# Strided attention scores of the odd layer: 64 by 64 tiles per head and class instead of 128-row products with zeros, and a row minimum taken in two steps

## The chip, the cores and the metric

The kernel runs on one core of a Trainium2 chip. The metric is the device time of one execution, in microseconds (us). Below, PE is the matrix engine (TensorE), DVE the vector engine, ACT the scalar engine, POOL GpSimd, and SP the queue that issues most DMAs. PSUM is the memory that PE writes; it is used here as eight banks of 128 partitions by 512 floats, four under the name `acc` and four under the name `w`.

## The reference

The network has two layers over 256 tokens of width 1024; each layer is a mixer followed by a squared-ReLU MLP, with RMS norms. The change is in the odd layer's mixer, a mixture of three dilated windows with 16 heads of width 64. Cut to what matters:

```
DIL_PAIRS = ((128, 1), (512, 4), (2048, 16))      # window, step; 3 groups
hcat = (xn @ w_in).reshape(b, s, 3, 3, 16, 64)    # group, q/k/v, head
q, k = rope(hcat[:, :, :, 0]), rope(hcat[:, :, :, 1]);  v = hcat[:, :, :, 2]
for each group g and token i:                     # keys i + offset, in steps of 1, 4, 16
    sc = q_g[i] . k_g[keys] * 64**-0.5            # keys outside 0..255 are masked
    o_g, lse_g = softmax(sc) @ v_g[keys], logsumexp(sc)
out = sum over g of softmax_g(lse_g) * o_g        # then out @ w_o
```

Because the three groups are mixed by their softmax denominators, one softmax over the keys of all three groups together gives the same result. That is how the kernel computes it.

## The kernel before

**Units.** Function `odd` goes over eight units, two heads each (j = 0 and 1). For a unit, `qk_steps` computes six 128-row products (q and k of the three groups, 64 rows per head) with the weights split in two float32r parts (`split`: ACT casts `whi`, DVE subtracts `wlo`, L201 and L202; `mm3`, L205 to L207, runs three products per weight tile), `rope` rotates them on ACT (L931, L932) and DVE (L934 to L944), and `value_steps` computes v. `attention` then computes scores and softmax, and `mix` (L1000, L1005) multiplies with v.

**Order of tokens.** The 256 tokens stand in an order in which the 64 tokens of equal residue modulo 4 follow each other, and in these 64 the four residues modulo 16. A token's keys in group 1 (step 4) and in group 2 (step 16) are therefore all in its own block of 64 tokens, called a class here. There are four classes: `i` (a tile of 128 queries) times `c` (a half of it).

**Scores.** For each (i, j) one bank `ss[i, j]` of kind `w` takes 384 columns: 256 of group 0 (`two_heads`, L214, two float32r products of 64 rows beside each other) and 128 of groups 1 and 2 (L967). For the latter, `q12` holds group 1 in partitions 0 to 63 and group 2 in 64 to 127. So that one product over 128 rows keeps the groups apart, `k12` is stored as a block diagonal with zeros in its other blocks: 64 columns of group 1, then 64 of group 2. Its two buffers are zeroed once by POOL (L877), and DVE writes the two blocks in two instructions (L944). L967 is a plain float32 product, as are L1000, L1005 and L283: each such matmul of the program stands in the trace as two MATMUL records. A form such as 128\*64 in a row is the part of the array that the product takes, rows by columns; 128x128 behind it is the moving operand, partitions by columns.

**Softmax.** For each (i, j) DVE adds the mask, scales, and takes the row's minimum of the negated scores in one instruction of 384 columns (L974, followed by the short record that reads its accumulator), ACT takes the exponential with the sum (L976), DVE the reciprocal (L977), and ACT scales (L978). `turn` transposes the 384 probabilities in three blocks on PE (L985, into a `w` bank), and ACT or DVE copies them out (L987).

**What sets the order.** `weave` interleaves the steps of one unit's attention with the projections of the next; in it the scores of unit u - 1 come first, then `other()`, which is `mix` of unit u - 2, then pauses, then the four turns between the projections' steps. Unit 0 and unit 7 have no `mix` behind their scores. Inside each engine's queue the framework's scheduler chooses the order from its own costs. The weights come through SP's queue, which waits for free buffers. The MLP after the odd layer follows `hand_over`.

Of the kernel before, what the change touches and what calls it, by code (L numbers as in the profile page):

```python
# [19 lines left out]
F32 = mybir.dt.float32  # L20
F32R = mybir.dt.float32r
AF = mybir.ActivationFunctionType
ALU = mybir.AluOpType
# [26 lines left out]
def trunk(ctx, tc, a, out):  # L50
# [100 lines left out]
    def cut(j, i, n):  # L151
        w = specs[j][1] // n
        return slice(i * w, (i + 1) * w)
# [55 lines left out]
    def two_heads(o, hi, lo, ts):  # L209

        for n, (y, z) in enumerate(((hi, hi), (hi, lo), (lo, hi))):
            for j in range(2):
                pb = slice(64 * j, 64 * j + 64)
                nc.tensor.matmul(o[j], y[pb, 0, ts], z[pb, 1, :], start=n == 0, stop=n == 2)  # L214
# [10 lines left out]
    def tok(t):  # L225
        return slice(t * P, (t + 1) * P)
# [638 lines left out]
    def odd(op, xT, s, late):  # L865
        xh, xl = xT
        cosT = op.tile([P, T], F32, name="cosT")
        sinT = op.tile([P, T], F32, name="sinT")
        mask = op.tile([P, NT, 384], F32, name="mask")
        for dst, nm in ((cosT, "cos_f"), (sinT, "sin_f"), (mask, "dil_mask")):  # L870
            nc.sync.dma_start(dst, a[nm])
        mixed = [quarter_pair("oa"), quarter_pair("ob")]

        k12 = []
        for i in range(2):
            z = op.tile([P, 2, 4, P], F32, name=f"k12_{i}")
            nc.gpsimd.memset(z, 0.0)  # L877
            k12.append(z)

        def unit_tiles(u):  # L880
            d = {"k12": k12[u % 2]}
            for n, shape, dt in (("q0h", [P, 2, T], F32R), ("q0l", [P, 2, T], F32R), ("q12", [P, 2, T], F32),
                                 ("v0", [P, NT, P], F32), ("v12", [P, 4, P], F32)):
                d[n] = op.tile(shape, dt, tag=n, name=n, bufs=2)
            return d

        def value_steps(d):

            wt, acc = [], {}

            def gemm(i, half):
                if len(wt) <= half:
                    wt.append(weight())
                first = i not in acc
                if first:
                    acc[i] = bank("acc")
                pq = acc[i]
                wh, wl = wt[half]
                for k in range(4):
                    ws = slice(k * 384, k * 384 + 384)  # L900
                    kk = 4 * half + k
                    mm3(pq[:, 0:384], xh[:, kk, tok(i)], xl[:, kk, tok(i)], wh[:, ws], wl[:, ws], first and k == 0, not first and k == 3)
            def out(i):
                pq, ri = acc[i], column(r[0], i)
                nc.vector.tensor_scalar(d["v0"][:, i, :], pq[:, 0:P], ri, None, ALU.mult)
                for c in range(2):
                    rows = slice(64 * c, 64 * c + 64)
                    nc.scalar.activation(d["v12"][0:64, 2 * i + c, :], pq[rows, P:2 * P], AF.Copy, scale=ri[rows])
                    nc.scalar.activation(d["v12"][64:P, 2 * i + c, :], pq[rows, 2 * P:3 * P], AF.Copy, scale=ri[rows])

            return [lambda i=i, h=h: gemm(i, h) for i in range(NT) for h in range(2)], [lambda i=i: out(i) for i in range(NT)]

        def qk_steps(d):


            hold = {}

            def gemm(b, f, half):
                if f == 0 and half == 0:
                    hold["w"], hold["p"] = weight(), bank("acc")  # L920
                (wh, wl), pq = hold["w"], hold["p"]
                for k in range(4 * half, 4 * half + 4):
                    ws = slice((f * KT + k) * P, (f * KT + k + 1) * P)
                    mm3(pq[:, f * T:(f + 1) * T], wh[:, ws], wl[:, ws], xh[:, k, :], xl[:, k, :], k == 0, k == KT - 1)
                if f == 1 and half == 1:
                    rope(b, pq)

            def rope(b, pq):
                sw, r1 = scratch([512], "sw"), scratch([2, T], "r1")
                for r in range(0, P, 64):  # L930
                    nc.scalar.copy(sw[r:r + 32], pq[r + 32:r + 64])  # L931
                    nc.scalar.copy(sw[r + 32:r + 64], pq[r:r + 32])  # L932
                sw = sw.rearrange("p (f n) -> p f n", f=2)
                nc.vector.tensor_tensor(r1, pq.rearrange("p (f n) -> p f n", f=2), cosT.unsqueeze(1).broadcast_to([P, 2, T]), op=ALU.mult)  # L934
                nc.vector.tensor_tensor(sw, sw, sinT.unsqueeze(1).broadcast_to([P, 2, T]), op=ALU.mult)
                if b == 0:
                    nc.vector.tensor_tensor(r1, r1, sw, op=ALU.add)
                    split(d["q0h"], d["q0l"], r1)
                elif b == 1:
                    nc.vector.tensor_tensor(d["q12"], r1, sw, op=ALU.add)  # L940
                else:
                    for r in (0, 64):
                        cut = lambda z: z[r:r + 64].rearrange("p j (c n) -> p j c n", n=64)
                        nc.vector.tensor_tensor(d["k12"][r:r + 64, :, :, r:r + 64], cut(r1), cut(sw), op=ALU.add)  # L944

            return [lambda v=(b, f, h): gemm(*v) for b in range(3) for f in range(2) for h in range(2)]

# [2 lines left out]
            return [g[0], lambda: run_all([g[1], o[0]]), g[2], lambda: run_all([g[3], o[1]])]  # L950

        turned = {}

        def attention(u, d, other, pause=2):


            probs = {}

            def scores():
                ss = {(i, j): bank("w") for i in range(NT) for j in range(2)}  # L960
                for i in range(NT):
                    two_heads([ss[i, j][:, 0:T] for j in range(2)], d["q0h"], d["q0l"], tok(i))
                for i in range(NT):
                    for j in range(2):
                        for c in range(2):
                            rows = slice(64 * c, 64 * c + 64)
                            nc.tensor.matmul(ss[i, j][rows, T:T + P], d["q12"][:, j, i * P + 64 * c:i * P + 64 * c + 64],  # L967
                                             d["k12"][:, j, 2 * i + c, :], start=True, stop=True)
                other()
                for i in range(NT):  # L970
                    for j in range(2):
                        sn, pp = scratch([384], "sn"), scratch([384], "pp")
                        mn, z, rz = (work.tile([P, 1], F32, tag=v, name=v, bufs=4) for v in ("dmn", "dz", "drz"))
                        nc.vector.tensor_tensor_reduce(out=sn, in0=ss[i, j][:, 0:384], in1=mask[:, i, :], op0=ALU.add, op1=ALU.min,  # L974
                                                       scale=-(HD ** -0.5), scalar=3e38, accum_out=mn)
                        nc.scalar.activation(pp, sn, AF.Exp, bias=mn, scale=-1.0, accum_out=z)  # L976
                        nc.vector.reciprocal(rz, z)  # L977
                        nc.scalar.activation(pp, pp, AF.Copy, scale=rz)  # L978
                        probs[i, j] = pp

            def turn(i, j):
                pp = probs.pop((i, j))
                pt = bank("w")
                for b in range(3):
                    nc.tensor.transpose(pt[:, b * P:(b + 1) * P], pp[:, b * P:(b + 1) * P], ident)  # L985
                pts = turned[u, i, j] = op.tile([P, 3, P], F32, tag="pts", name="pts", bufs=6)
                nc.any.tensor_copy(out=pts, in_=pt[:, 0:384].rearrange("p (b n) -> p b n", b=3))  # L987

            wait = lambda: None
            return [scores] + [wait] * pause + [f for i in range(NT) for j in range(2) for f in (lambda i=i, j=j: turn(i, j), wait)]  # L990
# [74 lines left out]
def _constants():  # L1065
    con = {}
    con["cos_r"], con["sin_r"] = _tables(32, ORDER)
    con["cos_f"], con["sin_f"] = (np.ascontiguousarray(np.tile(z.transpose(1, 0, 2).reshape(T, HD).T, (2, 1)))
                                  for z in _tables(HD, ORDER))
    q = ORDER.reshape(NT, P)  # L1070
    own = ORDER.reshape(4, 64).repeat(64, axis=0).reshape(NT, P, 64)
    ok0 = np.abs(q[:, :, None] - ORDER[None, None, :]) <= 64
    d = q[:, :, None] - own
    ok1 = (d % 4 == 0) & (np.abs(d) <= 256)
    ok2 = (d % 16 == 0) & (np.abs(d) <= 1024)
    m = np.where(np.concatenate([ok0, ok1, ok2], 2), 0.0, NEG).astype(np.float32)
    con["dil_mask"] = np.ascontiguousarray(m.transpose(1, 0, 2))
    return con

# [57 lines left out]
```

## Time and profile before

| | us |
|---|---|
| median of 3 runs | 737.83 (737.17 to 737.85) |
| the profiled execution, its time | 738.17 |
| its span | 736.4 |
| PE busy in the span | 727.2 (99%) |
| PE weight loads | 680.7 (92%) |
| DVE, ACT, POOL busy | 610.5 (83%), 558.9 (76%), 79.9 (11%) |
| the odd layer's strided scores, PE records of L967 | 128 records, 8.8 us |
| their softmax minimum, DVE L974 | 32 instructions, 17.5 us |
| writing k of groups 1 and 2, DVE L944 | 16 instructions, 10.9 us |

A row of the timeline gives the start, the time, the engine, the line, the operation, the tiles and how many records were merged; a bracket at its end names idle time before it and what ended that. Records of PE overlap, since matmuls are pipelined: the time from the start of one row to the start of the next is what a row costs. The granted clock of PE is 1.00 throughout the odd layer.

### The profile page before, as it was taken

The page shows a single profiled execution, that of the slowest core. Times are in us where ns is not written, and L with a number is a line of the kernel's source. Part 1 is how long each engine was busy: PE and PEld are TensorE (multiplying, and loading weights), DVE is VectorE, ACT ScalarE, POOL GpSimd, SP SyncE. Part 2 cuts the span into 40 slices and gives each one's busy share as a digit, 9 for nine tenths or more (in the row PEclk, how much of TensorE's full clock was granted, in tenths as well). Part 3 has the DMA queues.
Part 4 walks back from the last instruction along what each step waited for, and adds up shares of the span by engine and source line. Part 5 has one row for each costly group of instructions (what it writes and reads, how often), then busy time and mean ns, then how long its engine had stood idle before and what let it go on. Part 6 is the DMA issues. An engine that isn't in the chain of part 4 may idle for free.

```text
span 736.4 us, 14008 instructions
## 1 busy us (share of the span) xinstructions
PE 727.2 (99%) x5442; PEld 680.7 (92%) x5442; DVE 610.5 (83%) x1090; ACT 558.9 (76%) x1027; POOL 79.9 (11%) x75
## 2 busy tenths in 40 slices
PE   9999999999999999999999999999999999999996
PEld 6988899999999998999999999999999999999995
DVE  6888859999999959887778677776759999999957
ACT  7778968767766756888988989889867768767752
POOL 0100002224212000000000000000003123322000
PEclk9999999999999999999999999999999999999998
DMA  8773338798999643644443444534558699898611
GB/s 312 275 263 131 115 115 216 227 288 236 263 266 261 194 145 150 226 146 140 173 160 144 156 151 171 176 129 160 199 204 216 208 275 262 247 263 249 190 52 57
DMA packets 34178, 143.78 MB, mean 195 GB/s; under 512 B 3776, under 2 KB 5312, under 8 KB 25024
## 3 DMA queue, kind: packets, MB, share of 16 engines
q1 hardware_dynamic: 26208, 127.94, 49.6%
q0 software_dynamic: 7616, 14.68, 12.0%
q8 instruction: 42, 0.69, 0.4%
q10 hardware_dynamic: 288, 0.28, 0.1%
q14 instruction: 24, 0.20, 0.1%
HBM read 141.84 MB, written 1.05 MB: 194 GB/s over the span
## 4 chain that ended last, share of the span: by engine, by line
PE 92%; DVE 4%; ACT 1%; issue 1%; DMA 1%; POOL 0%; SPq 0%; POOLq 0%; DVEq 0%
PE acc L205 17%; PE acc L206 16%; PE acc L207 16%; PE w L205 11%; PE w L206 11%; PE w L207 11%; PE w L214 1%; PE w L985 1%; DVE wlo L202 1%; PE w L801 1%; PE w L967 1%; PE acc L1000 1%; PE w L815 1%; ACT whi L201 1%; DVE xl L242 1%
## 5 line engine op out<-in xcount | busy, mean ns | idle before, releaser
L202 DVE TENSOR_TENSOR wlo<-raw,whi 128x512 fp32r<-128x512 f32 (+3 forms) x360 | 297.0, 846 | 56.0 <-ACT whi L201 55.6
L201 ACT CAST whi<-raw 128x512 fp32r<-128x512 f32 (+3 forms) x360 | 253.8, 745 | 89.4 <-PE w L206 64.8
L206 PE MATMUL w<-xl,whi 128*128 128x256 f32 x528 | 149.6, 283 | 0.1
L207 PE MATMUL w<-xh,wlo 128*128 128x256 f32 x528 | 149.3, 283 | 0.0
L205 PE MATMUL w<-xh,whi 128*128 128x256 f32 x528 | 148.9, 283 | 0.0
L205 PE MATMUL acc<-xh,whi 128*128 128x256 f32 x432 | 125.2, 290 | 0.0
L206 PE MATMUL acc<-xl,whi 128*128 128x256 f32 x432 | 122.3, 283 | 0.0
L207 PE MATMUL acc<-xh,wlo 128*128 128x256 f32 x432 | 122.3, 283 | 0.0
L206 PEld LDWEIGHTS w<-xl,whi 128*128 128x128 f32 x528 | 101.2, 192 | 1.6 <-DVE xl L242 0.6
L205 PEld LDWEIGHTS w<-xh,whi 128*128 128x128 f32 x528 | 101.0, 192 | 1.0
L207 PEld LDWEIGHTS w<-xh,wlo 128*128 128x128 f32 x528 | 101.2, 192 | 0.0
L140 POOL COPY sum<-sum 128x512 f32<-128x512 f32 x28 | 41.4, 1494 | 468.3 <-DVE wlo L202 271.9
L205 PEld LDWEIGHTS acc<-xh,whi 128*128 128x128 f32 x432 | 82.5, 191 | 1.3 <-issue 0.3
L206 PEld LDWEIGHTS acc<-xl,whi 128*128 128x128 f32 x432 | 82.5, 191 | 0.0
L207 PEld LDWEIGHTS acc<-xh,wlo 128*128 128x128 f32 x432 | 82.4, 191 | 0.0
L205 PE MATMUL acc<-whi,xh 128*128 128x384 f32 (+2 forms) x160 | 55.4, 348 | 0.2 <-ACT whi L201 0.2
L206 PE MATMUL acc<-wlo,xh 128*128 128x384 f32 (+2 forms) x160 | 55.1, 344 | 0.4 <-DVE wlo L202 0.4
L207 PE MATMUL acc<-whi,xl 128*128 128x384 f32 (+2 forms) x160 | 54.7, 342 | 0.0
L201 ACT CAST hh<-h 128x896 fp32r<-128x896 f32 (+1 forms) x32 | 28.9, 903 | 18.2 <-DVE h L378 17.2
L205 PE MATMUL w<-whi,hh 128*128 128x512 f32 (+1 forms) x108 | 42.1, 390 | 0.0
L206 PE MATMUL w<-wlo,hh 128*128 128x512 f32 (+1 forms) x108 | 41.5, 384 | 0.0
L207 PE MATMUL w<-whi,hl 128*128 128x512 f32 (+1 forms) x108 | 41.2, 382 | 0.0
(225 smaller groups left out, 1495.4 us busy)
## 6 DMA issues: line engine op xcount, KB each, us to landing
raw<-in_w SPq DMA_DIRECT2D x36, 1024.0 KB, 5.4
raw<-in_w_oqk SPq DMA_DIRECT2D x24, 1024.0 KB, 4.8
raw<-in_w SPq DMA_DIRECT2D x28, 768.0 KB, 5.3
sum<-in_w POOLq DMA_DIRECT2D x28, 512.0 KB, 8.5
raw<-in_w_ov SPq DMA_DIRECT2D x16, 768.0 KB, 4.3
sum<-in_w SPq DMA_DIRECT2D x28, 256.0 KB, 6.1
raw<-in_w_oe SPq DMA_DIRECT2D x4, 1024.0 KB, 6.6
raw<-in_w_oo SPq DMA_DIRECT2D x4, 1024.0 KB, 4.8
```

The lines of the kernel that those rows point to most:

```text
L140: nc.gpsimd.tensor_copy(out=sums[:, 1, :], in_=sums[:, 0, :])
L201: a = nc.scalar.copy(hi, src).ins
L202: return a, (eng or nc.vector).tensor_tensor(lo, src, hi.bitcast(F32), op=ALU.subtract).ins
L205: nc.tensor.matmul(o, sh, mh, start=first, stop=False)
L206: nc.tensor.matmul(o, sh, ml, start=False, stop=False)
L207: nc.tensor.matmul(o, sl, mh, start=False, stop=last)
L214: nc.tensor.matmul(o[j], y[pb, 0, ts], z[pb, 1, :], start=n == 0, stop=n == 2)
L242: lambda: nc.vector.scalar_tensor_tensor(lo, v, gk, hi.bitcast(F32), ALU.mult, ALU.subtract).ins)
L801: nc.tensor.transpose(pt[:, b * P:(b + 1) * P], pp[:, b // 2, (b % 2) * P:(b % 2 + 1) * P], ident)
L815: nc.tensor.matmul(pvo[64 * j:64 * j + 64, 0:P], v[:, kk, h * 64:(h + 1) * 64], pts[:, 2 * j + kk, :], start=kk == 0, stop=kk == NT - 1)
L967: nc.tensor.matmul(ss[i, j][rows, T:T + P], d["q12"][:, j, i * P + 64 * c:i * P + 64 * c + 64], d["k12"][:, j, 2 * i + c, :], start=True, ...
L985: nc.tensor.transpose(pt[:, b * P:(b + 1) * P], pp[:, b * P:(b + 1) * P], ident)
```

## The change

The zeros are gone: `k12` becomes a tile like `q12` (group 1 in partitions 0 to 63, group 2 in 64 to 127, two buffers), written by one DVE instruction, and POOL's two memsets are dropped. The score of one class, head and group is a product of its own, 64 rows by 64 columns with a moving operand of 64 columns: 16 matmuls per unit where 8 were. The rows of the array that a product takes follow the group g, the columns follow c. Products of g = 0 go to bank `ss[i, 0]`, those of g = 1 to `ss[i, 1]`, whichever head they are of, at columns 0 to 63 for head 0 and 320 to 383 for head 1; group 0's scores move to columns 64 to 319. So head j's scores stand in 320 neighbouring columns of its own bank (256 of group 0 and one class block), and 64 more in the other head's bank. The minimum is taken in two steps: one instruction over the 320 columns, whose result `m0` is the starting value of a second one over the 64. The mask grows from 384 to 640 columns, so that both heads' orders are windows of it, and the places of groups 1 and 2 in v and the order of the three transposed blocks follow.

```diff
-        mask = op.tile([P, NT, 384], F32, name="mask")
+        mask = op.tile([P, NT, 640], F32, name="mask")
...
-        k12 = []
-        for i in range(2):
-            z = op.tile([P, 2, 4, P], F32, name=f"k12_{i}")
-            nc.gpsimd.memset(z, 0.0)
-            k12.append(z)
...
-                    for r in (0, 64):
-                        cut = lambda z: z[r:r + 64].rearrange("p j (c n) -> p j c n", n=64)
-                        nc.vector.tensor_tensor(d["k12"][r:r + 64, :, :, r:r + 64], cut(r1), cut(sw), op=ALU.add)
+                    nc.vector.tensor_tensor(d["q12" if b == 1 else "k12"], r1, sw, op=ALU.add)
...
+        END = (slice(0, 64), slice(320, 384))
...
-                    two_heads([ss[i, j][:, 0:T] for j in range(2)], d["q0h"], d["q0l"], tok(i))
+                    two_heads([ss[i, j][:, 64:64 + T] for j in range(2)], d["q0h"], d["q0l"], tok(i))
                 for i in range(NT):
                     for j in range(2):
                         for c in range(2):
-                            rows = slice(64 * c, 64 * c + 64)
-                            nc.tensor.matmul(ss[i, j][rows, T:T + P], d["q12"][:, j, i * P + 64 * c:i * P + 64 * c + 64],
-                                             d["k12"][:, j, 2 * i + c, :], start=True, stop=True)
+                            ts = slice(i * P + 64 * c, i * P + 64 * c + 64)
+                            for g in range(2):
+                                pb = slice(64 * g, 64 * g + 64)
+                                nc.tensor.matmul(ss[i, g][64 * c:64 * c + 64, END[j]], d["q12"][pb, j, ts], d["k12"][pb, j, ts],
+                                                 start=True, stop=True)
...
-                        nc.vector.tensor_tensor_reduce(out=sn, in0=ss[i, j][:, 0:384], in1=mask[:, i, :], op0=ALU.add, op1=ALU.min,
-                                                       scale=-(HD ** -0.5), scalar=3e38, accum_out=mn)
+                        low = 3e38
+                        for b, c, at, m in ((j, slice(64 * j, 64 * j + 320), slice(64 - 64 * j, 384 - 64 * j), m0), (1 - j, END[j], END[j], mn)):
+                            nc.vector.tensor_tensor_reduce(out=sn[:, at], in0=ss[i, b][:, c], in1=mask[:, i, T - T * j:640 - T * j][:, at], op0=ALU.add, op1=ALU.min,
+                                                           scale=-(HD ** -0.5), scalar=low, accum_out=m)
+                            low = m
...
-                for b in range(3):
-                    nc.tensor.transpose(pt[:, b * P:(b + 1) * P], pp[:, b * P:(b + 1) * P], ident)
+                for b, at in enumerate((0, P, T) if j else (P, T, 0)):
+                    nc.tensor.transpose(pt[:, b * P:(b + 1) * P], pp[:, at:at + P], ident)
```

In the built program the lines behind the change stand a few numbers lower: L967 becomes L962, L974 becomes L972, L976 to L978 become L975 to L977, L985 becomes L984, L987 becomes L986, L1000 and L1005 become L999 and L1004.

PE's queue keeps every other instruction at its place. At the scores of unit 1, followed by `mix` of unit 0, it stood before:

```order
L214 MATMUL w<-q0l,q0h 128x256 x2
L214 MATMUL w<-q0h,q0l 128x256 x2
L967 MATMUL w<-k_1_3458,q_3467 64x128 x8
L1000 MATMUL acc<-pts,v_3463 64x128 x4
L1005 MATMUL acc<-pts,v_3464 64x64 x4
L1000 MATMUL acc<-pts,v_3463 64x128 x4
L1005 MATMUL acc<-pts,v_3464 64x64 x4
L205 MATMUL acc<-xh,whi 128x256
```

And now (`k` and `q` are the tiles k12 and q12, `w` the score banks):

```order
L214 MATMUL w<-q0l,q0h 128x256 x2
L214 MATMUL w<-q0h,q0l 128x256 x2
L962 MATMUL w<-k_3465,q_3464 64x64 x16
L999 MATMUL acc<-pts,v_3460 64x128 x4
L1004 MATMUL acc<-pts,v_3461 64x64 x4
L999 MATMUL acc<-pts,v_3460 64x128 x4
L1004 MATMUL acc<-pts,v_3461 64x64 x4
L205 MATMUL acc<-xh,whi 128x256
```

Sixteen matmuls of 64 columns stand where eight of 128 stood.

DVE's queue at the softmax of unit 7, before (`wlo` are parts of the next weights, `ISA` with a 128x1 result reads the accumulator):

```order
L202 TENSOR_TENSOR wlo<-raw,whi 128x512 x4
L974 ISA sn,dmn<-w,mask 128x384
L974 ISA dmn 128x1
L202 TENSOR_TENSOR wlo<-raw,whi 128x512
L974 ISA sn,dmn<-w,mask 128x384
L974 ISA dmn 128x1
L977 RECIPROCAL drz<-dz 128x1
```

And now:

```order
L202 TENSOR_TENSOR wlo<-raw,whi 128x512 x5
L972 ISA sn,dm_6820<-w,mask 128x320
L972 ISA dm_6820 128x1
L972 ISA sn,dmn<-w,mask,dm_6820 128x64
L972 ISA dmn 128x1
L972 ISA sn,dm_6831<-w,mask 128x320
L972 ISA dm_6831 128x1
L972 ISA sn,dmn<-w,mask,dm_6831 128x64
L972 ISA dmn 128x1
L976 RECIPROCAL drz<-dz 128x1
```

One more `wlo` stands ahead of the first minimum, and each minimum is four rows instead of two.

ACT's queue at the softmax of unit 0, before:

```order
L201 CAST whi<-raw 128x384 x3
L976 ACTIVATE pp,dz<-sn,dmn 128x384
L201 CAST q0h<-r_3882 128x512
L976 ACTIVATE pp,dz<-sn,dmn 128x384
L978 ACTIVATE pp<-pp,drz 128x384 x2
```

And now:

```order
L201 CAST whi<-raw 128x384 x3
L201 CAST q0h<-r_3879 128x512
L975 ACTIVATE pp,dz<-sn,dmn 128x384
L977 ACTIVATE pp<-pp,drz 128x384
L975 ACTIVATE pp,dz<-sn,dmn 128x384
```

The cast of the next unit's q (`q0h`) now stands ahead of the first exponential. On POOL the two memsets are gone; SP's queue keeps its order.

14 lines of the change are left out of this document (6 added, 8 removed).

## The prediction

> **What bounds the kernel now.** I read the page first, then the busy time by stretches, then PE's timeline around one unit's scores, then the groups of DVE, then the timelines of DVE and ACT where PE waits.
>
> ```profile
> span 736.4 us, 14008 instructions
> PE 92%; DVE 4%; ACT 1%; issue 1%; DMA 1%; POOL 0%; SPq 0%; POOLq 0%; DVEq 0%
> 331.00:361.00 30.00, 30.00 (x263) 29.63 (x262) 21.26 (x46) 26.26 (x57) 0.00 (x0) 1.00 0.45 156
> ```
>
> The second line is the chain that ended last, by engine: 92% of it is PE. The third is the stretch 331 to 361 us, one unit of the odd layer: its columns are the length, then busy time of PE, PE's weight loads, DVE, ACT and POOL, the granted clock, the DMA share and GB/s. PE has no gap there; DVE has 8.7 us to spare and ACT 3.7. So in this layer a microsecond of PE's stream is a microsecond of the kernel, unless PE then waits for something else. This is PE at the scores of unit 1:
>
> ```profile
> 345.50 0.28 PE L207 MATMUL acc<-xh,wlo 128*128 128x256 f32 x1
> 345.71 0.39 PE L214 MATMUL w<-q0h 64*128 64x256 f32 x2
> ...
> 346.41 0.28 PE L214 MATMUL w<-q0h,q0l 64*128 64x256 f32 x2
> 346.62 1.09 PE L967 MATMUL w<-k,q 128*64 128x128 f32 x16
> 347.54 0.61 PE L1000 MATMUL acc<-pts,v 128*64 128x128 f32 x8
> 347.98 0.40 PE L1005 MATMUL acc<-pts,v 128*64 128x64 f32 x8
> 348.21 0.61 PE L1000 MATMUL acc<-pts,v 128*64 128x128 f32 x8
> 348.65 0.40 PE L1005 MATMUL acc<-pts,v 128*64 128x64 f32 x8
> 348.98 0.39 PE L205 MATMUL acc<-xh,whi 128*128 128x256 f32 x1
> ```
>
> These are the same kind of product over the whole array, and the scores of unit 7 with no `mix` behind them:
>
> ```profile
> 300.31 0.71 PE L283 MATMUL w<-diag,mean 128*128 128x128 f32 x4 [0.23 <-DVE diag L276]
> 300.78 0.37 PE L206 MATMUL acc<-xl,whi 128*128 128x256 f32 x1
> ...
> 530.43 1.09 PE L967 MATMUL w<-k,q 128*64 128x128 f32 x16
> 531.45 0.38 PE L205 MATMUL acc<-oah,whi 128*128 128x256 f32 x1
> ```
>
> Over the whole array four float32 records of 128 columns take 0.47 us, 118 ns each. L967's 16 records of as many columns take 0.92, 58 ns each: the two halves of the columns (c = 0 and 1) work beside each other. L1000's eight take 0.44, that is 0.109 per pair; so L967 is 8 x 0.109 = 0.87 and 0.05 at its start. L1005's eight records of 64 columns take 0.23: 58 ns per pair. A change of the array's form costs 0.10: L967 in front of a 128\*128 product takes 1.02 instead of 0.92, and L1005 0.33 instead of 0.23. L214's pairs, two halves of the rows in two banks, also run together: two records end within the 0.28 of one.
>
> **PE's part of the change.** A unit's 16 records of 128 columns become 32 of 64. The trace has pairs by columns and pairs by rows, and no product of 64\*64. If four run at a time, which the two pairings suggest, a unit takes 8 steps of 58 ns = 0.46, plus 0.05 at the start and some 0.02 until the last of four is off. If two run at a time it is 16 x 58 ns = 0.93. Those are the ends short of no overlap at all (32 x 58 ns = 1.86). I take four, since both directions of pairing are there in rows, and the products of the two row halves go to two banks, as L214's do. The page TensorEngine Tiling (Array Packing) of the Trainium skill (section Key Properties) says that tiles operate independently and that a change of mode drains the array; the 0.10 us above agree with the drain, and no run here shows the four tiles.
>
> Before, L967 and `mix` had the same form, 128\*64. Now 64\*64 stands ahead of 128\*64, so in the six units with a `mix` there is one more change of form (0.10) and one more start (0.05). Units 1 to 6: 0.05 + 0.46 + 0.02 + 0.10 + 0.05 = 0.68 instead of 0.92, a gain of 0.24 each. Units 0 and 7, where the change of form was there already: 0.63 instead of 1.02, a gain of 0.39 each. By PE's stream alone that is 6 x 0.24 + 2 x 0.39 = 2.2 us.
>
> **DVE's part.**
>
> ```profile
> L974 DVE CUSTOM_DVE_ANT_0 sn<-w,mask 128x384 f32<-128x384 f32 x32 | 17.5, 546 | 0.0
> L944 DVE TENSOR_TENSOR k<-r,sw 64x512 f32<-64x512 f32 x16 | 10.9, 684 | 0.1
> L786 DVE CUSTOM_DVE_ANT_0 sn<-w,bias 128x256 f32<-128x256 f32 x16 | 6.3, 421 | 1.4 <-PE w L214 1.4
> L940 DVE TENSOR_TENSOR q<-r,sw 128x512 f32<-128x512 f32 x8 | 5.5, 685 | 0.0
> ```
>
> The same instruction takes 421 ns on 256 columns and 546 on 384, 0.98 ns a column. From one start to the next the 384 cost 0.48 (533.25 to 533.73 below), so 320 cost 0.42 and 64 cost 0.17, and the accumulator's read is 0.08. The second step needs the first one's result: I put 0.05 for that, the nearest row being ACT's start 0.03 after such a read; the ends are 0 and 0.3. Per unit DVE gets 4 x (0.42 + 0.08 + 0.05 + 0.17 + 0.08 - 0.56) = 1.0 more and loses one of two L944 of 0.60, since the whole 128x512 (L940) takes as long as half of it. 0.4 us in 8.7 of slack cost nothing by themselves; what counts is the delay of a unit's first turn on PE.
>
> Unit 1 has room: its first probabilities are scaled at 352.24 to 352.86, and the turn comes at 354.83. Units 2 to 6 repeat it.
>
> ```profile
> 352.24 0.62 ACT L978 ACTIVATE pp<-pp,drz 128x384 f32<-128x384 f32 x1
> 354.83 0.49 PE L985 MATMUL w<-ident,pp 128*128 128x128 f32 x3
> ```
>
> There each first minimum comes one `wlo` (0.6) and one more step later, about 0.9 us in all against 2.0. Nothing is lost. A bank of scores is now read by both heads, so it comes free one head later; that is still before the scaling that the turn waits for.
>
> Unit 7 has no room; it waits already:
>
> ```profile
> 532.64 0.69 DVE L202 TENSOR_TENSOR wlo<-raw,whi 128x512 fp32r<-128x512 f32 x1 [0.82 <-ACT whi L201]
> 533.25 0.55 DVE L974 CUSTOM_DVE_ANT_0 sn<-w,mask 128x384 f32<-128x384 f32 x1
> 533.73 0.08 DVE L974 DVE_READ_ACCUMULATOR2_ANT dmn<- 128x1 f32 x1
> ...
> 533.84 0.62 ACT L976 ACTIVATE pp<-sn,dmn 128x384 f32<-128x384 f32 x1 [0.71 <-DVE dmn L974]
> 534.92 0.62 ACT L976 ACTIVATE pp<-sn,dmn 128x384 f32<-128x384 f32 x1 [0.37 <-DVE dmn L974]
> 535.54 1.11 ACT L978 ACTIVATE pp<-pp,drz 128x384 f32<-128x384 f32 x2
> ...
> 535.74 0.28 PE L207 MATMUL acc<-oah,wlo 128*128 128x256 f32 x1
> 536.19 0.55 PE L985 MATMUL w<-ident,pp 128*128 128x128 f32 x3 [0.17 <-ACT pp L978]
> ```
>
> PE could turn at 535.86 (0.12 after the L207) and does at 536.19. The order there is both exponentials, then both scalings. Now a second `wlo` stands at 533.25 and the first minimum starts at 533.86: 320 columns to 534.28, read to 534.36, wait to 534.41, 64 columns and read to 534.66. The second head follows the same way from 534.58 and is done at 535.38, so the second exponential starts at 535.41 instead of 534.92, and the turn 0.49 later, at 536.68. PE comes 0.39 earlier and waits that too. Unit 7 thus costs 0.49 where its stream alone would have gained 0.39. Without the extra `wlo` it would cost nothing; with waits of 0.3 in each step it would cost 1.0.
>
> Unit 0 stands close:
>
> ```profile
> 325.59 0.69 DVE L937 TENSOR_TENSOR r<-r,sw 128x512 f32<-128x512 f32 x1
> 327.20 0.68 DVE L202 TENSOR_TENSOR q0l<-r,q0h 128x512 fp32r<-128x512 f32 x1
> ...
> 326.32 0.61 ACT L201 CAST q0h<-r 128x512 fp32r<-128x512 f32 x1
> 326.83 0.62 ACT L976 ACTIVATE pp<-sn,dmn 128x384 f32<-128x384 f32 x1
> 327.44 1.16 ACT L978 ACTIVATE pp<-pp,drz 128x384 f32<-128x384 f32 x2
> ...
> 328.79 0.49 PE L985 MATMUL w<-ident,pp 128*128 128x128 f32 x3
> ```
>
> The first exponential moves behind the cast of `q0h`, to 326.8. DVE's reciprocal then stands behind one `wlo`, the next minimum's first step and `q0l`, and is done at 328.0 where the scaling began at 327.44. With 0.65 from scaling to turn as in unit 7, the turn is ready at 328.65; PE would be there at 328.79 - 0.39 = 328.40. Unit 0 keeps 0.14.
>
> **What costs nothing.** The mask's DMA grows by 256 KB and POOL loses two memsets:
>
> ```profile
> 278.21 0.42 SPq L871 DMA_DIRECT2D mask<-in_dil_mask x1
> 293.07 0.33 SPq L147 DMA_DIRECT2D raw<-in_w_oqk x1
> 298.83 1.10 POOL L265 TENSOR_TENSOR rstd<-ms,mhalf 128x2 f32<-128x2 f32 x1 [22.37 <-DVE ms L259]
> ```
>
> Behind the mask SP's queue stands still for 14 us until a buffer is free, which covers the larger transfer; the mask is first read at unit 0's softmax, near 325. POOL had been idle for 22 us ahead of its next work, so the memsets hid nothing and delayed nothing.
>
> **The sum.** 6 x 0.24 + 0.14 - 0.49 = 1.09 us less. Against the profiled execution that is 738.17 - 1.09 = 737.1; the median of the runs stands 0.34 below that execution, so I forecast 737.83 - 1.09 = 736.7.
>
> **The rivals.**
> Two at a time: a record cannot start sooner than 29 ns after the one before, whichever tile it goes to, or the four tiles do not overlap. For it speaks that 29 ns is the closest mean spacing in any row; against it that L214's two records start within 10 ns. Units 1 to 6 then take 0.05 + 0.93 + 0.10 + 0.05 = 1.13, 0.21 more than now, unit 0 0.06 more, unit 7 0.49 more as above: 1.8 us slower, 739.6. It decides from a mean spacing of about 22 ns on: there 32 records take 0.70, the six units gain nothing and unit 7's loss is left.
> A floor between them: with 25 ns per record, 32 take 0.80, units 1 to 6 lose 0.08 each, unit 0 keeps 0.07, unit 7 loses 0.49: 738.7. The page TensorE: Matmul & The Clock Gate of the Trainium skill (section Wait — 56ns, not 53.3ns?) says that start-to-start never drops below about 25 ns however small the product; L214's rows differ from it.
> No stall: DVE and ACT reach units 0 and 7 earlier than I put them, and all 2.2 us arrive: 735.6. For it speaks that the `wlo` order decides it; against it that unit 7 waits already.
> A new stall in units 1 to 6: the softmax would have to come 2 us later, twice what I count; 0.2 in each of the six puts the time at 737.9.
> No overlap at all: 32 x 58 ns costs 1.14 more in units 1 to 6, 0.99 in unit 0, and unit 7's turn comes 0.66 later: 746.3. The pairs in the rows speak against it.
>
> **How the numbers follow.** The forecast, 736.7 with 735.9 to 737.5 as its own range, has a chance of 58%. No stall has 13%, two at a time 14%, the floor of 25 ns 6%, a new stall 6%, no overlap 3%. The range from 735.4 to 739.3 leaves out a part of the first, most of two at a time and no overlap, 18 in 100. A change of 0.2%, 1.5 us, is about what a measurement of this kernel can tell from none: faster is below 736.35 (no stall and over a quarter of the forecast, 0.29), slower above 739.3 (most of two at a time, no overlap, a little of a new stall, 0.17), the rest is within.
>
> **What would show it.** L962 before L999 in one unit: about 0.63 us from start to start if four run at a time, 1.08 if two. The strided minimum: 64-column steps of about 0.17 us, and L934 for k of 685 ns once per unit. Unit 7's first turn should have a longer wait for ACT, over 1 us behind the product ahead of it, and unit 0's about 0.25; the other units none. The prediction is wrong if the form 64\*64 has a cost of its own beyond a change of form, or if a unit that had 2 us of room turns late.

## The result, and the profile after

| | before | after |
|---|---|---|
| median of 4 runs each, same chip | 737.84 us (737.17 to 738.1) | 743.8 us (743.44 to 744.27) |
| span of the profiled execution | 736.4 | 741.6 |

The change makes the kernel slower: 1.0081 times the time before, 95% interval 1.0069 to 1.0094, where 736.7 was forecast. The page of the changed kernel gives the span and the chain that ended last, by engine:

```profile
span 741.6 us, 14330 instructions
PE 67%; ACT 16%; DVE 12%; issue 4%; DMA 1%; POOL 0%; SPq 0%; POOLq 0%; DVEq 0%
```

PE carried 92% of that chain before. Now 28% of it runs through ACT and DVE. To see where the time went, I cut both spans at the same four matrix products of PE: one near the start of the first MLP, one at its end, one behind the odd layer and one near the end of the second MLP. The stretches are the first MLP, the odd layer and most of the second MLP. Columns: length, then busy time and records of PE, PE's loads, DVE, ACT and POOL, the granted clock, the DMA share, GB/s. Before:

```profile
125.04:295.12 170.08, 170.08 (x1096) 155.98 (x1095) 156.43 (x214) 118.93 (x165) 33.08 (x24) 1.00 0.76 225
295.12:560.18 265.06, 264.58 (x2301) 260.26 (x2301) 197.84 (x412) 224.83 (x469) 6.17 (x7) 1.00 0.49 168
560.18:729.05 168.87, 168.87 (x1112) 155.32 (x1112) 155.10 (x199) 114.46 (x148) 30.68 (x23) 1.00 0.71 205
```

After:

```profile
124.23:295.95 171.72, 171.72 (x1095) 156.09 (x1094) 156.92 (x214) 119.13 (x165) 29.48 (x22) 1.00 0.75 225
295.95:564.05 268.10, 264.45 (x2430) 257.29 (x2429) 197.35 (x469) 225.30 (x468) 6.16 (x7) 1.00 0.48 166
564.05:734.37 170.32, 170.32 (x1112) 155.25 (x1112) 155.35 (x199) 114.66 (x148) 30.14 (x23) 1.00 0.70 203
```

There are two losses. The odd layer is 3.04 us longer, and PE idles 3.65 us in it (0.48 before). The two MLPs, in which the change touches nothing, are 1.64 and 1.45 us longer although PE is full in both kernels, with the same products and the same clock. The stretch ahead of the first MLP, from 6 us on, is 118.2 us long instead of 118.9, which lies within what it varies by among the executions of kernels with the addresses of before (118.1 to 119.3).

PE's timeline at the scores of unit 1, and the first row of scores in units 3, 4 and 5:

```profile
347.44 0.69 PE L962 MATMUL w<-k,q 64*64 64x64 f32 x32
348.07 0.66 PE L999 MATMUL acc<-pts,v 128*64 128x128 f32 x8
...
407.63 0.69 PE L962 MATMUL w<-k,q 64*64 64x64 f32 x32
438.43 0.69 PE L962 MATMUL w<-k,q 64*64 64x64 f32 x32
469.20 0.69 PE L962 MATMUL w<-k,q 64*64 64x64 f32 x32
```

L962 takes 0.63 from start to start: the products themselves are as fast as forecast. But units 3 and 4, from scores to scores, last 30.80 and 30.77 us, where PE's own stream before was 30.35 (the scores of units 3 to 6 start at 407.32, 437.68, 468.03 and 498.38) less 0.24. The softmax of unit 4 in both kernels, first before, with PE's scores, DVE and ACT:

```profile
437.68 1.09 PE L967 MATMUL w<-k,q 128*64 128x128 f32 x16
440.55 0.55 DVE L974 CUSTOM_DVE_ANT_0 sn<-w,mask 128x384 f32<-128x384 f32 x1
441.30 0.61 ACT L976 ACTIVATE pp<-sn,dmn 128x384 f32<-128x384 f32 x1
```

And after (the score row is above):

```profile
442.20 1.29 DVE L202 TENSOR_TENSOR wlo<-raw,whi 128x512 fp32r<-128x512 f32 x2 [0.96 <-ACT whi L201]
443.41 0.48 DVE L972 CUSTOM_DVE_ANT_0 sn<-w,mask 128x320 f32<-128x320 f32 x1
443.82 0.08 DVE L972 DVE_READ_ACCUMULATOR2_ANT dm<- 128x1 f32 x1
443.82 0.69 DVE L202 TENSOR_TENSOR wlo<-raw,whi 128x512 fp32r<-128x512 f32 x1
444.43 0.27 DVE L972 CUSTOM_DVE_ANT_0 sn<-w,mask,dm 128x64 f32<-128x64 f32 x1
444.63 0.08 DVE L972 DVE_READ_ACCUMULATOR2_ANT dmn<- 128x1 f32 x1
...
444.74 0.62 ACT L975 ACTIVATE pp<-sn,dmn 128x384 f32<-128x384 f32 x1 [1.01 <-DVE dmn L972]
```

Before, the first minimum starts 2.87 us behind the scores and the exponential 3.62. Now it is 4.98 and 6.31, a `wlo` stands between the two steps of one minimum, and ACT stands idle for 1.01 us in front of an exponential whose minimum is not there. In unit 1 the first minimum still came at 351.04, 3.60 behind its scores; it falls back 0.7 us per unit (4.33 in unit 2, 5.00 in unit 3) until PE waits too:

```profile
461.25 0.44 PE L206 MATMUL acc<-wlo,xh 128*128 128x384 f32 x1 [0.23 <-DVE wlo L202]
535.39 0.39 PE L205 MATMUL acc<-oah,whi 128*128 128x256 f32 x1 [1.43 <-ACT v L903]
540.20 0.55 PE L984 MATMUL w<-ident,pp 128*128 128x128 f32 x3 [0.98 <-ACT pp L977]
```

PE waits for `wlo` inside a unit and, in unit 7, for ACT's copies of v and for the first turn. DVE and ACT wait for each other, as the view of waits from 330 to 555 us has it (us in total, times, the longest):

```profile
DVE wlo L202 <- ACT whi L201: 26.7, 17, 4.0
DVE r L928 <- ACT sw L926: 24.7, 19, 2.3
ACT v L902 <- DVE v L899: 12.8, 7, 1.8
...
ACT pp L975 <- DVE dmn L972: 7.8, 7, 1.7
```

### The profile page after: what moved, and what is told of

Same layout as the page of the kernel before. It is cut to its first block, busy times and chain, and to the rows that moved or that the text cites. A ratio compares the mean times of both kernels' runs of the same rounds, so it can differ in the third digit from the quotient of the medians.

```text
span 741.6 us, 14330 instructions
## 1 busy us (share of the span) xinstructions
PE 729.8 (98%) x5570; PEld 677.6 (91%) x5570; DVE 610.4 (82%) x1147; ACT 559.8 (75%) x1026; POOL 76.0 (10%) x73
## 4 chain that ended last, share of the span: by engine, by line
PE 67%; ACT 16%; DVE 12%; issue 4%; DMA 1%; POOL 0%; SPq 0%; POOLq 0%; DVEq 0%
PE w L206 12%; PE w L205 12%; PE w L207 12%; PE acc L205 9%; PE acc L206 9%; PE acc L207 9%; DVE wlo L202 5%; ACT whi L201 4%; ACT sw L925 3%; ACT sw L926 3%; ACT pp L975 2%; DVE sn L972 2%; ACT pp L977 2%; ACT v L903 1%; DVE sw L929 1%
## 5 line engine op out<-in xcount | busy, mean ns | idle before, releaser
L206 PEld LDWEIGHTS w<-xl,whi 128*128 128x128 f32 x528 | 99.3, 188 | 1.5 <-DVE xl L242 0.3
L207 PEld LDWEIGHTS w<-xh,wlo 128*128 128x128 f32 x528 | 99.7, 189 | 0.0
L140 POOL COPY sum<-sum 128x512 f32<-128x512 f32 x28 | 39.4, 1421 | 473.0 <-DVE wlo L202 276.6
L928 DVE TENSOR_TENSOR r<-acc,cosT 128x512 f32<-128x512 f32 x24 | 16.6, 691 | 29.4 <-ACT sw L926 29.4
```

The costliest lines, as they stand in the source:

```text
L140: nc.gpsimd.tensor_copy(out=sums[:, 1, :], in_=sums[:, 0, :])
L206: nc.tensor.matmul(o, sh, ml, start=False, stop=False)
L207: nc.tensor.matmul(o, sl, mh, start=False, stop=last)
```

## The experiments

Each kernel ran in turns with the kernel before. The odd layer below is always the stretch between the same two products as above.

| | us | ratio, 95% | odd layer |
|---|---|---|---|
| after | 743.8 | 1.0069 to 1.0094 | 268.10 |
| e1 before, 128 bytes | 740.1 | 1.0020 to 1.0043 | 264.70 |
| e2 after, no tile moved | 741.59 | 1.0036 to 1.0066 | 268.15 |
| e3 before, two steps | 741.69 | 1.0040 to 1.0070 | 268.71 |
| e4 e2, second step free | 738.02 | 0.9994 to 1.0013 | 264.92 |
| e13 e2, order repaired | 736.6 | 0.9974 to 0.9993 | 263.63 |
| e16 before, same order | 737.65 | 0.9990 to 1.0009 | 264.63 |
| e7 before, 64 bytes | 730.06 | 0.9877 to 0.9906 | 263.52 |
| e15 e13, 64 bytes | 727.56 | 0.9848 to 0.9878 | 260.28 |

### Addresses: e1 and e2

The new tile `dm0` has four buffers of 32 bytes per partition in the pool `work`. Every tile allocated behind it, `raw`, `whi` and `wlo` among them, starts 128 bytes later, while `x`, `xh` and `hh` stay.

```diff
# e1, in the kernel before
-        turned = {}
+        turned, pad = {}, work.tile([P, 32], F32, name="pad", bufs=1)
# e2, in the changed kernel
-                        m0, mn, z, rz = (work.tile([P, 1], F32, tag=v, name=v, bufs=4) for v in ("dm0", "dmn", "dz", "drz"))
+                        mm = work.tile([P, 2], F32, tag="dmn", name="dmn", bufs=4)
+                        m0, mn = mm[:, 0:1], mm[:, 1:2]
+                        z, rz = (work.tile([P, 1], F32, tag=v, name=v, bufs=4) for v in ("dz", "drz"))
```

> The kernel before with one unused tile of 128 bytes per partition ahead of the raw weight buffers; every queue keeps its order. It moves raw, whi, wlo and all later tiles by 128 bytes against x, xh, xl and hh, as the new dm0 tile of the changed kernel does. Theory A (addresses): in the two MLPs a product of 512 columns takes 0.233 us instead of 0.227 and these stages lose 1.6 and 1.5 us, the first layer gains about 0.8; 737.8 + 2.3 = 740.1 us. Rival B (the slower MLPs of the changed kernel come from its other edits, or from the execution): spacing stays at 0.227, 737.8 us with 0.7 either way.

> The changed kernel with m0 and mn as two columns of one tile, so that no tile outside the odd layer moves. Theory A: the MLPs' products of 512 columns are back at 0.227 us and the time is 743.8 - 2.3 = 741.5 us. Rival B: 743.8. The odd layer keeps its loss under both: the softmax of units 3 to 6 falls behind and the first turn waits for ACT.

Measured: 740.1 and 741.59, as theory A had it (740.1 and 741.5). The two MLPs of e1, then of e2:

```profile
124.30:296.03 171.73, 171.73 (x1096) 156.07 (x1094) 156.46 (x214) 119.20 (x165) 32.01 (x24) 1.00 0.74 223
560.73:731.21 170.48, 170.48 (x1112) 155.40 (x1112) 154.95 (x199) 114.79 (x148) 32.70 (x23) 1.00 0.70 203
```

```profile
124.64:294.67 170.03, 170.03 (x1096) 155.97 (x1095) 155.86 (x214) 118.66 (x165) 32.08 (x22) 1.00 0.75 227
562.82:731.67 168.85, 168.85 (x1111) 155.29 (x1112) 154.90 (x199) 114.67 (x148) 31.07 (x23) 1.00 0.70 205
```

So 2.2 us of the 6.0 come from the place of a four-byte tile: some 3.1 in the MLPs, of which the other stages give a part back (e1's odd layer is 0.4 shorter than before). The rest, 3.8, is the odd layer.

### The two steps: e3 and e4

```diff
# e3, in the kernel before (m0 and mn as in e2)
-                        nc.vector.tensor_tensor_reduce(out=sn, in0=ss[i, j][:, 0:384], in1=mask[:, i, :], ..., scalar=3e38, accum_out=mn)
+                        low = 3e38
+                        for at, m in ((slice(0, 320), m0), (slice(320, 384), mn)):
+                            nc.vector.tensor_tensor_reduce(out=sn[:, at], in0=ss[i, j][:, at], in1=mask[:, i, at], ..., scalar=low, accum_out=m)
+                            low = m
# e4, in e2
-                            low = m
-                        nc.scalar.activation(pp, sn, AF.Exp, bias=mn, scale=-1.0, accum_out=z)
+                        nc.scalar.activation(pp, sn, AF.Exp, bias=m0, scale=-1.0, accum_out=z)
```

> The kernel before with the minimum in two dependent steps of 320 and 64 columns of the same bank; scores, zeros and addresses stay as before. Theory C (the two dependent steps alone make the softmax late, ACT idle and PE wait): the odd layer loses what it lost in the changed kernel beside PE's gain, 3.1 + 2.2 = 5.3 us: 743.1. Rival D (the loss needs the 64 by 64 products or the scores shared between two banks): four times 0.4 us of DVE per unit hide, 737.8 to 738.5. MLP spacing 0.227 under both.

> The kernel of the second experiment with a second step that does not wait for the first: it starts from 3e38, and the exponential takes the minimum of the first 320 columns alone (the 64 others are left out of the minimum). DVE does the same instructions. Theory C1 (what costs is the dependence, with the wlo that the scheduler puts between the two steps and ahead of the exponential): the exponentials come as early as before, the odd layer gains PE's 2.2 us and keeps at most unit 7's loss: 736 to 737.5. Rival C2 (DVE's extra instructions cost, wherever they stand): 741, as without the edit.

Measured: 741.69 and 738.02, the first between the two theories' times and nearer to C's 743.1, the second above the 736 to 737.5 of C1. Two steps alone, with the old products, cost 4.0 us; the shared banks and the 64 by 64 products are not needed for the loss. Without the dependence 3.6 of e2's loss are gone, but PE's gain does not arrive. Of e4, the scores of units 2 and 6, the first minimum behind each, and PE's waits in unit 7:

```profile
376.63 0.58 PE L962 MATMUL w<-k,q 64*64 64x64 f32 x24
380.61 0.48 DVE L974 CUSTOM_DVE_ANT_0 sn<-w,mask 128x320 f32<-128x320 f32 x1
497.08 0.69 PE L962 MATMUL w<-k,q 64*64 64x64 f32 x32
501.40 0.48 DVE L974 CUSTOM_DVE_ANT_0 sn<-w,mask 128x320 f32<-128x320 f32 x1
531.71 0.38 PE L205 MATMUL acc<-oah,whi 128*128 128x256 f32 x1 [1.22 <-ACT v L903]
536.09 0.55 PE L985 MATMUL w<-ident,pp 128*128 128x128 f32 x3 [0.52 <-ACT pp L978]
```

Four units take 120.45, so PE runs at its own 30.11 each, all of the 0.24 kept. But the minimum moves from 3.98 to 4.32 behind the scores, 0.09 per unit: ACT and DVE need 30.20 for a unit, and in unit 7 PE waits for them and gives the gain back. By the waits above that is a loop: DVE waits for ACT's `whi` and `sw`, ACT for DVE's minimum and v, each in the order of its queue, so the idle time of neither is free.

### Relief for the loop: e5, e6, e9 and e10

```diff
# e5 in e2, e6 in the kernel before
         raw, hi, lo = (z[:, cut(j, i, n)] for z in parts[j][:3])
+        if odd_at <= j < odd_at + 40 and i == 3:
+            eng = nc.gpsimd
# e9 in e2, e10 in the kernel before: v12 on DVE, four times
-                    nc.scalar.activation(d["v12"][...], pq[rows, ...], AF.Copy, scale=ri[rows])
+                    nc.vector.tensor_scalar(d["v12"][...], pq[rows, ...], ri[rows], None, ALU.mult)
```

> The kernel of the second experiment with every fourth wlo of the odd layer's weights (5 of 20 per unit) on POOL, which is idle there; DVE then has no wlo between the two steps. Theory L (ACT and DVE wait for each other in a loop that runs through a unit: 30.80 us per unit in the changed kernel, 30.20 with the free second step, against PE's own 30.11): DVE gets 3 us per unit less, the loop falls below PE's 30.11, units 1 to 6 keep their 0.24 each and only unit 7 can lose: 735.5 to 737. Rival M (what costs is the later exponential by itself, through the banks and the turn, whatever else DVE does; or POOL's wlo comes late): 740 to 742.

> The kernel before with the same wlo on POOL, to see what that alone does. Theory L: PE's stream bounds the odd layer before the change, so only the waits at unit 7 (about 0.5 us) can go: 737.2 to 737.7. Rival M: a gain of as much as the fifth experiment shows against the second would mean that POOL's help is worth something without the 64 by 64 products.

Measured: 750.25 and 754.62, both wide of either theory: DVE was not relieved. Two of DVE's groups in e5 (line, shape, count, busy us, mean ns, idle before), and two rows of its timeline:

```profile
L205 DVE TENSOR_TENSOR wlo<-raw,whi 128x512 fp32r<-128x512 f32 x54 | 47.3, 902 | 15.7 <-ACT whi L204 15.7
L937 DVE TENSOR_TENSOR q<-r,sw 128x512 f32<-128x512 f32 x6 | 9.1, 1509 | 0.0
...
372.15 1.17 POOL L205 TENSOR_TENSOR wlo<-raw,whi 128x384 fp32r<-128x384 f32 x1 [5.48 <-ACT whi L204]
372.36 1.51 DVE L937 TENSOR_TENSOR q<-r,sw 128x512 f32<-128x512 f32 x1
```

A `q` takes 1509 ns, where it took 685, when it starts beside a `wlo` of POOL, and DVE's `wlo` take 902 in the mean instead of 686. The page SBUF — State Buffer of the Trainium skill (section Summary: rules for kernel authors) says that of a DVE operation with two SBUF inputs and a GpSimd operation that reads SBUF the second one to issue blocks until the first is done; the trace agrees: this `q` starts 0.21 us behind POOL's `wlo` and ends at 373.87, 0.55 behind POOL's end at 373.32. These two runs say nothing about the loop.

> The kernel of the second experiment with the eight copies of v12 per unit on DVE instead of ACT, without POOL: ACT gets 8 times 0.37 = 3.0 us per unit less, DVE some 2 us more, and ACT no longer waits for DVE's v (1.9 us per unit in the fourth experiment's trace). Theory L (the loop of ACT and DVE is the bound once PE's unit falls below it): the loop falls below PE's 30.11 us, units 1 to 6 keep 0.24 each, unit 7 at least a part: 735.3 to 737. Rival M (the late exponential by itself costs): 740 to 742, as without the edit.

> The kernel before with the same copies on DVE. Theory L: before the change PE's unit of 30.35 us already is the longer one, so the shorter loop brings only the waits at unit 7, at most 0.5 us: 737.2 to 737.8. Rival: a gain as large as the ninth experiment's against the second would mean that the copies cost by themselves.

Measured: 738.79 and 737.5, the second as expected. In e9 the loss of e2 shrinks by 2.8 us, but not to the 735 to 737 expected. The softmax still falls back by 0.35 per unit, half of the 0.7: ACT, now with less to do, waits 5.2 us per unit (30.9 in six units) for DVE's minimum. The load of one engine was not the whole of it; its order was left.

### Faster products: e7, e8, e11, e12 and e14

e7 and e8 are e1 with 64 and 256 bytes. e11 is e9, and e14 is e10, with 64 bytes. e12 is e9 with 64 bytes in the pool of constants, ahead of `x`:

```diff
# e12
+    const.tile([P, 16], F32, name="pad")
```

> The kernel before with an unused tile of 64 bytes per partition in the place of the first experiment's 128. Theory A1 (what matters is the start address of the tiles modulo 256 or less): the MLPs' products of 512 columns take another time than 0.227 and 0.233; by the 128 bytes' 2.4 us, between 736.5 and 741. Rival A2 (any move off the old place costs the same): 740.1.

> The same with 256 bytes. Theory A1 (modulo 256 or less): as with no pad, 737.7. Rival A2 (any move costs): 740.1. Theory A3 (a longer period, 512 bytes or more): a third value.

> The ninth experiment's kernel with the 64 bytes placed ahead of x, so that xl, xh and hh too start at a multiple of 128 bytes. Theory A1 (a product is slow where the tile it streams or loads does not start at a multiple of 128): the products of 512 columns, which stream hh, also come to their shortest, 0.227 or less, and the time is 0.5 to 3 us under the eleventh experiment's. Rival A4 (only the distance between the two operands counts): x and raw keep their old distance, so the times are the ninth experiment's, about 736.

Measured: 730.06, 737.6 and 738.91. A shift of 64 bytes makes the kernel before 7.6 us faster, which neither expectation of e7 had; 256 bytes do nothing. e12 has the time of e9 (738.79), while e11, with the same 64 bytes behind `x`, `xh` and `hh`, has 731.42 (below): where these move along, nothing changes. So the place of the weights' tiles by itself does not decide; what fits all these runs is the distance between the two groups. `x`, `xh` and `hh` were never moved alone, and which accesses meet there is not shown. The MLPs of e7, and the first of e12:

```profile
123.24:291.16 167.92, 167.92 (x1096) 152.93 (x1095) 156.41 (x215) 119.42 (x165) 33.36 (x24) 1.00 0.75 229
554.68:721.03 166.35, 166.35 (x1111) 152.01 (x1112) 154.70 (x199) 114.48 (x148) 33.36 (x23) 1.00 0.72 207
```

```profile
125.00:295.07 170.07, 170.07 (x1095) 155.95 (x1094) 155.60 (x214) 118.21 (x165) 31.04 (x22) 1.00 0.74 227
```

e7 also measures the loop of the kernel before, since PE is now faster than it. Its scores of units 1, 2, 5 and 6:

```profile
341.08 1.09 PE L967 MATMUL w<-k,q 128*64 128x128 f32 x16
370.64 0.55 PE L967 MATMUL w<-k,q 128*64 128x128 f32 x6
...
460.72 1.09 PE L967 MATMUL w<-k,q 128*64 128x128 f32 x16
491.02 1.09 PE L967 MATMUL w<-k,q 128*64 128x128 f32 x16
```

PE's own unit is 29.56; once the softmax has used up its lead, the unit is 30.24 to 30.30. e1 agrees without faster products: its units are 30.31, and its first minimum comes nearer to the scores by 0.05 per unit (2.93 behind them in unit 2, 2.76 in unit 5), so its loop is about 30.26. So before the change the loop of ACT and DVE was 0.05 to 0.1 us shorter than PE's unit of 30.35, and not 3.7 or 8.7.

> The ninth experiment's kernel with the 64 bytes of the seventh. In the seventh, PE's unit was 29.57 us while its softmax fell behind and then 30.3, so that 2 to 3 us of PE's gain in the odd layer were lost to the loop. Theory L: with the shorter loop these and PE's 2.2 us come too: 725.5 to 727.5. Rival: the loop is no shorter, 730 or more.

> The kernel before with v12 on DVE and the 64 bytes of the seventh experiment. Theory L: with faster products PE's unit is 29.57 us and the loop is the bound; v12 on DVE shortens the loop from 30.27, so the time falls below the seventh's 730.06, to 727 to 729.5. Rival: the loop is as long or longer with the copies on DVE: 730 to 732.

Measured: 731.42 and 728.36. In e11 the loop holds PE at 30.43 per unit and the rival is right. In e14 PE keeps its 29.56 through all of units 1 to 5 while the first minimum falls back 0.28 per unit: a loop of 29.84, worth 1.7 us against e7.

### The order: e13, e15 to e18

In e13 the scheduler must issue the last four `wlo` of units 1 to 6 behind the second step of the second tile. No instruction and no dependence for data changes.

```diff
# e13, in e2 (pieces collects the wlo instructions of split_piece)
+                        if i == 0 and j == 1 and 0 < u < 7:
+                            for w in pieces[-4:]:
+                                tc.add_manual_dep(w, step.ins.name, mybir.DependencyInfo(mybir.DependencyClass.NoSync, mybir.DependencyReason.DATA), reason="order")
```

> The kernel of the second experiment in which units 1 to 6 issue the last four wlo on DVE behind the minima of the first two tiles, so that nothing stands between their steps and the exponentials find their minima earlier. Instructions and dependences are the same. Theory T2 (the order of the queues around the two steps made the loop of ACT and DVE 30.80 us long): the loop comes near the 30.2 of the free step, and the time near its 738.0: 737 to 739. Rival T1 (the dependence itself, wherever the wlo stand): 741.6 as without the edit, or more if the wlo are now late for PE.

Measured: 736.6, a little under the range of T2 and 5.0 under e2. PE's scores and DVE in unit 6 of e13, and its chain by engine:

```profile
496.45 0.69 PE L965 MATMUL w<-k,q 64*64 64x64 f32 x32
496.96 0.49 DVE L977 CUSTOM_DVE_ANT_0 sn<-w,mask 128x320 f32<-128x320 f32 x1 [2.38 <-PE w L965]
497.38 0.08 DVE L977 DVE_READ_ACCUMULATOR2_ANT dmn<- 128x1 f32 x1
497.60 0.28 DVE L977 CUSTOM_DVE_ANT_0 sn<-w,mask,dmn 128x64 f32<-128x64 f32 x1
497.81 0.08 DVE L977 DVE_READ_ACCUMULATOR2_ANT dmn<- 128x1 f32 x1
...
498.55 2.50 DVE L205 TENSOR_TENSOR wlo<-raw,whi 128x512 fp32r<-128x512 f32 x4
```

```profile
PE 93%; DVE 3%; ACT 2%; issue 1%; POOL 0%; POOLq 0%; DVEq 0%
```

DVE now waits for the scores (2.38) and not ACT for DVE. In units 1 to 6 the first minimum starts 0.51 behind the scores, nothing falls back, each of units 1 to 6 keeps its 0.24, and PE carries the chain again. Unit 7 still has DVE's order of e2 around its softmax, yet from its scores to the end of the odd layer it takes 29.84 instead of 31.78: what it lost was the delay brought in from the units before. So the order of the queues made the loss, and T1 fell. The run moves four `wlo` at once and leaves others between the steps of the later tiles, so it does not say what each place costs.

> The kernel before with the order of the thirteenth experiment (in units 1 to 6 the last four wlo behind the first two minima), one-step minimum, zeros kept. If PE's stream bounds the odd layer there, the order brings nothing: 737.3 to 738. Rival: the order itself is worth the 1.1 us by which the thirteenth was faster: 736.6.

> The thirteenth experiment's kernel with the 64 bytes. Theory L: PE's unit would be 29.33 us, so the odd layer runs at the loop's period. If T2 holds and the loop is near 30.2: 729.5 to 730.5, level with the seventh. If T1 holds: 733 to 734 (30.8 per unit). In no case does the 64 by 64 product's own gain show, since PE is not the bound there.

> The same with the 64 bytes of the seventh experiment. With the order the loop of ACT and DVE should come under PE's unit of 29.57 us, so the odd layer runs at PE's pace: by units 3 to 6 at 0.7 us each under the seventh, 727 to 728. The fifteenth, with the 64 by 64 products, had 727.56; if PE bounds both, this one is 0.5 to 2 us slower than that, if the loop still bounds both, level.

> The fifteenth experiment's kernel with the order also in unit 7, whose first minimum came 4.4 us behind its scores and should now come 0.5 behind. The first turn of unit 7 then no longer waits for ACT: 0.5 to 1.5 us less than 727.56. Rival: unit 7's waits are for ACT's copies of v12 and its casts, which the order does not move: 727.5.

Measured: e16 737.65, e15 727.56, e17 730.66 (0.9893 to 0.9926), e18 726.28 (0.9828 to 0.9884). The order alone gives the kernel before nothing, so e13's gain over it belongs to the products. With 64 bytes, e15 runs its units at 29.51, PE's own pace, while the first exponential falls back 0.16 per unit: the order brought the loop from 30.80 to 29.67. e15 came out below its expectation, which had supposed a loop near 30.2. e17 reaches 30.28 and misses its 727 to 728: there the same rule does not shorten the loop. I have no run that tells why. One difference that the traces show is that e17 still writes k in two DVE instructions ahead of v (1.38 us for the two), e15 in one (0.69); whether that is the reason is not tested. e18 and e15 are level within their intervals, so e18 does not decide between its two expectations. They are the fastest kernels here, 10 to 11 us under the kernel before and 16 to 17.5 under the changed one; 7.6 of that is what 64 bytes do alone.

## Why the prediction was wrong, point by point

**PE's part was right.** Four tiles run at a time: 0.63 from L962 to L999 as forecast, 32 records in about 0.46, which is 14 ns a record; in the trace they start in fours, 7 ns apart inside a four and 58 ns from one four to the next. The page TensorE: Matmul & The Clock Gate of the Trainium skill (section Wait — 56ns, not 53.3ns?) gives a floor of about 25 ns from start to start; for these four tiles the measurement decides against it, so "two at a time", "a floor between them" and "no overlap at all" fell. The 0.24 per unit arrives in full in e4 and e13.

**The durations of DVE were nearly right.** In e13 the 64-column step takes 0.21 from its start to that of its read where I allowed 0.17, and it starts 0.14 after the read before it where I put 0.05; a minimum in two steps takes 0.93 (496.96 to 497.89) instead of 0.80. That is not the error.

**The step that failed is "Nothing is lost" in units 1 to 6**, with "0.4 us in 8.7 of slack cost nothing". I read the delay right for unit 1 (the first minimum 3.60 behind the scores, 0.65 more than before) and then wrote that units 2 to 6 repeat it. They do not. Idle time of DVE and ACT in that stretch was mutual waiting; e7 shows their loop at 30.24 to 30.30, where PE's unit was 30.35. With a `wlo` ahead of and between the two steps it became 30.80, so that the delay grew by 0.7 a unit, used the 2.0 us of room by unit 3, and cost PE about 0.65 in each of units 3 to 6. "A new stall in units 1 to 6" was among the rivals, with the condition that came true (the softmax 2 us late: 2.1 in unit 4), but with 6% and 0.2 us per unit. The prediction's own sign of being wrong, "a unit that had 2 us of room turns late", came: units 3 to 6 turned late.

**Unit 7** was priced as a turn 0.49 later. The turn does wait (0.98 after, 0.17 before), but in front of it a product of the next stage waits 1.43 for ACT's copies of v, which the prediction did not look at; ACT is late there for the same reason, since e13 has no such wait. From unit 7's scores to the end of the stretch it came to 1.93 us (31.68 after, 29.75 before). **Unit 0** lost 0.28 of its 0.39 and kept 0.11 up to its first turn; forecast 0.14. By unit 1's scores 0.01 of it was left.

**"What costs nothing"** treated the mask and the memsets, and those cost nothing that a run shows. It left out the new four-byte tile, whose place cost 3.1 us in the MLPs (e1, e2).

The sum, then: for the odd layer -1.09 was forecast and +3.04 measured, and for the MLPs 0 was forecast and +3.09 measured. Of the 4.13 by which the odd layer misses, 2.6 are units 1 to 6 (-1.44 forecast; units 1 and 2 gained 0.29 and 0.22, units 3 to 6 lost 0.44, 0.42, 0.45 and 0.32), 1.4 unit 7 (+0.49 forecast) and 0.1 unit 0. With the order repaired and no tile moved (e13) the change has 736.6. That this is the number forecast is in part luck: there unit 7 costs 0.09 and not 0.49, and the odd layer is 1.43 shorter and not 1.09. For the kernel that was run the forecast is wrong.

## What to carry to other kernels

Idle time of two engines that wait for each other in fixed queues is not slack. Measure their loop by making the bound engine faster and seeing where the unit's length stops falling, and look for a delay that grows from unit to unit, not only at the first one. When one instruction becomes two dependent ones, look in the built order at what the scheduler puts between them. And when a small edit changes the time of a stage that it does not touch, compare the start addresses of the tiles first.

## What the hardware showed that I had not expected

The distance in memory between the weights' tiles and `x`, `xh` and `hh`, as far as these runs go, changes the pace of PE's products: 128 bytes more made the MLPs 1.0% longer (1.65 and 1.61 us in e1), 64 bytes made the kernel 7.6 us faster with no other edit, 256 bytes did nothing, and moving both groups by 64 did nothing either. A subtraction on POOL beside it more than doubled DVE's `q`, 685 to 1509 ns. Four 64 by 64 tiles ran beside each other in full: 32 records of 64 columns took about 0.46 us, where the same columns took 0.87 with two tiles beside each other.
